# Key norms, bonus sums, merge banks and gate blocks of a hybrid decoder block put in another order on one core

## The chip, the cores and the metric

The kernel runs on one core of one Trainium2 chip. The metric is the time of one execution on the device, in microseconds (us); the median of several runs is compared. The engines of a core have a queue of instructions each and meet at semaphores: TensorE (PE, matmuls; its weight loads are PEld), VectorE (DVE), ScalarE (ACT), GpSimd (POOL), and SyncE (SP), on whose queue this kernel issues its DMAs.

## What is computed

A decoder block for 1024 tokens of width 1024. A conditioning vector gives shift, scale and gate for two sub-layers. The first sub-layer runs two token mixers on one normalised input and merges them by gates; the second is a SwiGLU feed-forward part.

```python
ada = (c @ ada_w[l] + ada_b[l])[:, None, :]
shift1, scale1, gate1, shift2, scale2, gate2 = jnp.split(ada, 6, axis=-1)
h = rms_norm(x, norm1_gain[l]) * (1 + scale1) + shift1
proj = jnp.einsum('bsd,de->bse', h, w_in[l])
rwkv_cols = proj[..., :q_lo]
rwkv_cols = rwkv_cols + (token_shift(rwkv_cols) - rwkv_cols) * tshift_mu[l]
y_a = rwkv7_time_mix(rwkv_cols, ...)
y_b = sliding_window_sink_attention(...)
gates = jax.nn.sigmoid(proj[..., g_lo:] + branch_gate_b[l])
merged = gate_a * (y_a @ w_branch_a[l]) + gate_b * (y_b @ w_branch_b[l])
x = x + gate1 * (merged @ w_out[l])
h2 = rms_norm(x, norm2_gain[l]) * (1 + scale2) + shift2
x = x + gate2 * ((jax.nn.silu(h2 @ ffn_w1[l]) * (h2 @ ffn_w3[l])) @ ffn_w2[l])
```

Inside the recurrent mixer (8 heads of 64 channels), the part that the change touches first:

```python
kk = heads(k * k_k).astype(f32)
kk = kk / jnp.maximum(jnp.sqrt(jnp.sum(kk * kk, axis=-1, keepdims=True)), 1e-12)   # key norm
k = k * (1 + (a - 1) * k_a)
y = wkv7_scan(rh, heads(decay), kh, vh, -kk, kk * ah)
bonus = jnp.sum((rh * kh * r_k).astype(f32), axis=-1, keepdims=True) * vh.astype(f32)
return (yn + bonus).reshape(B_, S_, W).astype(cols.dtype) * g
```

## The kernel before

Matrix products of float32 data are made of three matmuls on a high and a low part (`mm3`, L140 to L144). A weight block is loaded and split by `load_split`: `whi` on ACT (L133), `wlo` on VectorE (L134).

The tokens are worked on in two halves (h=0 and 1) of 512. In each half four recurrent *units* (p=0 to 3, two heads each) are formed, then an attention projection and four attention blocks, and 16 *gate blocks* (L945 to L951): a projection block of 24 matmuls, a tanh `gt` on ACT, and a store to `gates_d`, whose issue stands on SP.

A unit takes three projection blocks of 24 matmuls each, in the order k, r, v. `shifted` (L483) ends each: `tm` on ACT (L489), `rvk` on VectorE (L491). Then `rwkv_unit` (L494) is written out:

- `pz` and `paa` on PE (L499, L505), `sz` and `ath` on ACT, a scan `cum` on VectorE (L511), `wpad` and `winv` on ACT (L515, L517): the decays.
- The key norm: the square `sq` on ACT (L522), the column sum `ns` on PE (L524), `nrow` on ACT, two short DMAs by way of `n_scr`, and a reciprocal `inv2`, which the solve reads.
- `ar`, `aw`, `kp` and `kb` on VectorE (L538 to L554), with a copy of half of `kb` on ACT (L555).
- `rk`, written into the tile of `ath` (L558); the bonus sum `bs` on PE (L561) and its product with v, `bv` (L563), which only the end of the unit reads.
- The matmuls `pa` (L574), which read `kb` and `ar`; transposes `pk` and `pvt`; a triangular solve on VectorE (L605 to L625), and a loop over eight chunks (L659 to L701).

`ns`, `bs` and `pa` all write PSUM tiles of the pool `pm`, which has two buffers.

Behind each unit, `ada_rest` (L875) forms an eighth of what is left of the conditioning: eight rounds of a DMA of weights (issued on SP, L883), a product `adaw` on ACT (L884) and a sum on POOL (L885). All rounds use one buffer (`adaw2`, bufs=1), so a round's DMA is issued when POOL has done with the round before.

After the mixers, `branch` projects the two mixers' outputs and merges them with the gates, read back from `gates_d` into tiles also named `gt`. Its banks come from `pg2` (6 buffers); `psg` (L976) is a small product that spreads a gate of the conditioning, in `pn2` (2 buffers). The feed-forward part works by sums of blocks; `hidden_first` (L1272) is the first step for a pair of hidden columns: the weights are split into `wpart` (`split`, L1052), two products, and copies `u` on ACT (L1278).

A scheduler decides the order of instructions on each engine, by its own model of their times and the program's order; code under `tc.high_priority()` is put ahead of what stands before it where its data allow. The queues then run in that order.

Of the kernel before, what the change touches and what calls it, by code (L numbers as in the profile page):

```python
# [19 lines left out]
P = 128  # L20
# [7 lines left out]
NPOOL = 3  # L28
NC = HALF // 64
# [37 lines left out]
def block_kernel(ctx: ExitStack, tc: tile.TileContext, a: dict, out: bass.AP):  # L67
# [109 lines left out]
    with ExitStack() as mx:  # L177
# [316 lines left out]
        def rwkv_unit(h, p, rvk, xwa, sgx):  # L494
# [25 lines left out]

            sq = wk.tile([P, HALF], F32, tag="early", name="sq", bufs=5)
            nc.scalar.activation(out=sq, in_=k_, func=AF.Square, scale=vcol("k_k", p))  # L522
            ns = pm.tile([2, HALF], F32, tag="pm", name="ns")
            nc.tensor.matmul(ns, lhsT=blk1[:, 0:P:64], rhs=sq, start=True, stop=True)  # L524
            nrow = wk.tile([2, HALF], F32, tag="early", name="nrow", bufs=5)
            nc.scalar.copy(out=nrow, in_=ns)
            nc.sync.dma_start(out=n_scr[h, p], in_=nrow)
            inv2 = wk.tile([P, 32], F32, tag="inv2", name="inv2", bufs=2)
            nc.sync.dma_start(out=inv2, in_=n_scr[h, p].rearrange("q (c t) -> (q c) t", t=32)
                              .unsqueeze(0).broadcast_to([4, 32, 32]))  # L530
            nc.vector.tensor_scalar(out=inv2, in0=inv2, scalar1=1e-24, scalar2=None, op0=ALU.max)
            nc.vector.reciprocal(out=inv2, in_=inv2)
# [35 lines left out]
            for b in range(2):  # L568
# [325 lines left out]

        for h in range(NH):
            if h == 0:
# [20 lines left out]
            for p in range(NP):  # L917
                mixer_step(h, p, hT)
                rvk = wk.tile([P, 3, HALF], F32, tag="rvk", name="rvk", bufs=2)
                for i, j in ((2, 4 + p), (0, p), (1, 8 + p)):  # L920
                    shifted(hT, j, rvk[:, i, :])
                rwkv_unit(h, p, rvk, xwa, sgx)
# [4 lines left out]
                ada_rest(4 * h + p)  # L927

# [16 lines left out]
            for j in range(16):  # L945
                ps = proj_block(hT, 20 + j)
                gt = mw.tile([P, HALF + 1], F32, tag="tm", name="gt", bufs=3)

                nc.scalar.activation(out=gt[:, 0:HALF], in_=ps, func=AF.Tanh, scale=0.5,
                                     bias=hbg[:, j:j + 1])  # L950
                nc.sync.dma_start(out=gates_d[h, j], in_=gt[:, 0:HALF])  # L951
# [3 lines left out]
    with ExitStack() as fx:  # L955
        wp2 = fx.enter_context(tc.tile_pool(name="wp2", bufs=1))
        xp = fx.enter_context(tc.tile_pool(name="xp", bufs=1))
        wsets[:] = [wsets[0], wsets[0], (wp2, "2", 1, 1)]
        pg = fx.enter_context(tc.tile_pool(name="pg2", bufs=6, space=PSUM))
        pn = fx.enter_context(tc.tile_pool(name="pn2", bufs=2, space=PSUM))  # L960
# [252 lines left out]
        ysa[1] = load_y(ya_d, 1, lambda: st_tile("yst"))  # L1213
# [40 lines left out]
        def product(ps, w, bs, first, last):  # L1254
            hi, lo = split(w)
# [88 lines left out]
        def first(jp):  # L1344
            return hidden_first(jp, load13(jp))[0]
# [124 lines left out]
```

## Time and profile before

| what | value |
|---|---|
| timed runs | 1656.13, 1649.59, 1655.84 us, median 1655.84 |
| the profiled execution | 1638.24 us, span 1636.5 us |
| granted TensorE clock, mean | 0.989 |
| PE, PEld, DVE, ACT, POOL busy | 95%, 73%, 73%, 43%, 10% of the span |

The span is the profiled program on the core, the time has a little around it. [...] An idle time is put down to the semaphore that came last.

### The profile page before, as it was taken

How to read it: one execution, taken by the hardware profiler on the slowest of the kernel's cores; microseconds unless marked ns; L12 is line 12 of the kernel's file. 1: busy time of each engine (PE TensorE's matmuls, PEld its weight loads, DVE VectorE, ACT ScalarE, POOL GpSimd, SP SyncE). 2: the span in 40 equal slices, each digit the busy share in tenths (PEclk: the TensorE clock that was granted, in tenths of full speed). 3: DMA queues.
4: the chain of work that ended last, by engine and by line, in shares of the span. 5: the costliest groups of instructions: out<-in, count | busy, mean ns of one | idle time of the engine just before them, and what ended most of it. 6: DMA issues, size and time to landing. Idle time of an engine off the chain costs nothing.

```text
span 1636.5 us, 24815 instructions
## 1 busy us (share of the span) xinstructions
PE 1553.0 (95%) x8835; PEld 1195.9 (73%) x8835; DVE 1192.2 (73%) x2844; ACT 709.1 (43%) x1346; POOL 156.1 (10%) x220
## 2 busy tenths in 40 slices
PE   3978999999998999999999998999999999999998
PEld 2756776666665678667778886788888888888887
DVE  6689777877557868877368877976666677897465
ACT  6454343555744333446411566423333333444442
POOL 6223121212343000000000000000000000000000
PEclk9999999999999999999999999999999999999999
DMA  9345444544544323324583146253333232974441
GB/s 320 101 120 146 123 139 121 155 128 145 152 139 112 85 69 95 99 86 146 167 282 119 59 157 223 87 171 104 103 97 104 97 102 94 313 242 131 149 142 52
DMA packets 225502, 223.97 MB, mean 137 GB/s; under 512 B 38466, under 2 KB 162508, under 8 KB 225380
## 3 DMA queue, kind: packets, MB, share of 16 engines
q1 hardware_dynamic: 225380, 222.41, 44.4%
q8 instruction: 69, 1.13, 0.3%
q14 instruction: 53, 0.43, 0.1%
HBM read 171.73 MB, written 50.63 MB: 136 GB/s over the span
## 4 chain that ended last, share of the span: by engine, by line
PE 73%; DVE 11%; DMA 6%; ACT 4%; issue 2%; POOL 2%; SPq 1%; ACTq 0%; DVEq 0%; POOLq 0%
PE pgf L142 10%; PE pgf L143 10%; PE pgf L144 10%; PE pgo L144 6%; PE pgo L143 6%; PE pgo L142 6%; DMA adaw<-in_ada_w_dram 4%; PE pg L142 4%; PE pg L143 4%; PE pg L144 4%; PE pgq L142 1%; PE pgq L144 1%; PE pgq L143 1%; DVE rt L623 1%; DVE tmpi L619 1%
## 5 line engine op out<-in xcount | busy, mean ns | idle before, releaser
L142 PE MATMUL pg<-hhi,wlo 128*128 128x512 f32 x480 | 201.0, 421 | 2.0 <-DVE xwa L491 0.9
L143 PE MATMUL pg<-hlo,whi 128*128 128x512 f32 x480 | 198.8, 414 | 0.0
L144 PE MATMUL pg<-hhi,whi 128*128 128x512 f32 x480 | 198.2, 413 | 0.0
L144 PE MATMUL pgo<-wpart 128*128 128x512 f32 x420 | 163.9, 390 | 0.0
L143 PE MATMUL pgo<-wpart 128*128 128x512 f32 x420 | 163.8, 390 | 0.0
L142 PE MATMUL pgo<-wpart 128*128 128x512 f32 x420 | 163.3, 390 | 0.0
L133 ACT CAST whi<-wraw 128x1024 fp32r<-128x1024 f32 (+1 forms) x88 | 85.0, 967 | 98.2 <-PE pgf L144 45.0
L134 DVE TENSOR_TENSOR wlo<-wraw,whi 128x1024 fp32r<-128x1024 f32 (+1 forms) x88 | 100.9, 1146 | 26.0 <-ACT whi L133 18.0
L885 POOL TENSOR_TENSOR aacc<-aacc,adaw 128x512 f32<-128x512 f32 x64 | 90.6, 1416 | 257.6 <-ACT adaw L884 246.8
L142 PEld LDWEIGHTS pg<-hhi,wlo 128*128 128x128 f32 x480 | 92.5, 193 | 28.4 <-issue 6.7
L1066 DVE TENSOR_TENSOR u<-pgf,u 128x512 f32<-128x512 f32 x88 | 60.5, 689 | 68.0 <-PE pgf L144 67.1
L144 PEld LDWEIGHTS pg<-hhi,whi 128*128 128x128 f32 x480 | 92.8, 193 | 22.2 <-issue 3.3
L143 PEld LDWEIGHTS pg<-hlo,whi 128*128 128x128 f32 x480 | 92.9, 193 | 19.2 <-issue 1.3
L1061 ACT CAST wpart<-s 128x512 fp32r<-128x512 f32 x88 | 54.7, 622 | 111.0 <-PE pgf L144 99.8
L1061 ACT CAST wpart<-fo 128x512 fp32r<-128x512 f32 x77 | 48.0, 624 | 113.9 <-PE pgo L144 107.9
L1062 DVE TENSOR_TENSOR wpart<-fo,wpart 128x512 fp32r<-128x512 f32 x77 | 52.8, 687 | 52.4 <-ACT wpart L1061 52.3
L143 PEld LDWEIGHTS pgo<-wpart 128*128 128x128 f32 x420 | 78.8, 188 | 16.3 <-issue 0.2
L144 PEld LDWEIGHTS pgo<-wpart 128*128 128x128 f32 x420 | 78.9, 188 | 16.2
L142 PEld LDWEIGHTS pgo<-wpart 128*128 128x128 f32 x420 | 78.8, 188 | 16.2
L1061 ACT CAST wpart<-wraw 128x512 fp32r<-128x512 f32 x66 | 40.6, 622 | 101.3 <-PE pgf L144 98.6
L619 DVE SCALAR_TENSOR_TENSOR tmpi<-ai,inv,rt 128x60 f32<-128x60 f32 (+24 forms) x248 | 74.3, 300 | 10.6 <-DMA ai<-a_scr 6.9
L884 ACT ACTIVATE adaw<-adaw,vT 128x512 f32<-128x512 f32 x64 | 46.2, 722 | 73.2 <-DMA adaw<-in_ada_w_dram 67.7
(507 smaller groups left out, 3807.3 us busy)
## 6 DMA issues: line engine op xcount, KB each, us to landing
wraw<-in_w_in_dram SPq DMA_DIRECT2D x72, 512.0 KB
wraw<-in_ffn_w_dram SPq DMA_DIRECT2D x56, 512.0 KB
f_d<-fs SPq DMA_DIRECT2D x77, 256.0 KB
fo<-f_d SPq DMA_DIRECT2D x77, 256.0 KB
adaw<-in_ada_w_dram SPq DMA_DIRECT2D x64, 256.0 KB
w2t<-in_ffn_w_dram SPq DMA_DIRECT2D x44, 256.0 KB
adaw<-in_ada_w_dram SPq DMA_DIRECT2D x8, 1024.0 KB
gates_d<-gt SPq DMA_DIRECT2D x32, 256.0 KB
```

Source lines behind the costliest of these rows:

```text
L133: nc.scalar.copy(out=hi, in_=raw)
L134: nc.vector.tensor_tensor(out=lo, in0=raw, in1=hi.bitcast(F32), op=ALU.subtract)
L142: nc.tensor.matmul(ps, lhsT=ll, rhs=rh, start=first, stop=False, skip_group_check=more)
L143: nc.tensor.matmul(ps, lhsT=lh, rhs=rl, start=False, stop=False, skip_group_check=more)
L144: nc.tensor.matmul(ps, lhsT=lh, rhs=rh, start=False, stop=last, skip_group_check=more)
L619: nc.vector.scalar_tensor_tensor(out=tv, in0=ai[:, jj, j + 1:32].unsqueeze(1).broadcast_to([P, m, n]), scalar=inv2[:, j:j + 1], in1=rt[:, ...
L623: nc.vector.tensor_tensor(out=rt[:, 0:m, j + 1:32], in0=rt[:, 0:m, j + 1:32], in1=tv, op=ALU.add)
L884: nc.scalar.activation(out=wt, in_=wt, func=AF.Copy, scale=vcol("c", k))
L885: nc.gpsimd.tensor_tensor(out=acc, in0=acc, in1=wt, op=ALU.add)
L1061: nc.scalar.copy(out=hi, in_=src)
L1062: nc.vector.tensor_tensor(out=lo, in0=src, in1=hi.bitcast(F32), op=ALU.subtract)
L1066: nc.vector.tensor_tensor(out=out, in0=x, in1=y, op=op)
```

## The change

Five things are done, and the instructions stay the same in number and kind.

1. The square of the keys (`key_square`) is written right behind the k projection, and the rest of the key norm (`key_norm`) behind the r projection, ahead of v and of `rwkv_unit`.
2. `bs` and `bv` are written behind the loop of `pa`.
3. Three gate blocks of h=0 are written between units: one behind unit p=0, two behind p=1 (`GATES_BETWEEN`); the other 13 stay where they were.
4. The PSUM pool `pn2` is opened ahead of `pg2`, which swaps their banks.
5. In the merge, the load and split of `ysa[1]`, and in the first hidden step of the first three column pairs the splits and the `u` copies, are put under `high_priority`.

```diff
+GATES_BETWEEN = ((1, 2, 0, 0), (0, 0, 0, 0))
...
+        def key_square(p, k_):
+
+            sq = wk.tile([P, HALF], F32, tag="early", name="sq", bufs=5)
+            nc.scalar.activation(out=sq, in_=k_, func=AF.Square, scale=vcol("k_k", p))
+            return sq
+
+        def key_norm(h, p, sq):
+
+            ns = pm.tile([2, HALF], F32, tag="pm", name="ns")
+            nc.tensor.matmul(ns, lhsT=blk1[:, 0:P:64], rhs=sq, start=True, stop=True)
+            nrow = wk.tile([2, HALF], F32, tag="early", name="nrow", bufs=5)
+            nc.scalar.copy(out=nrow, in_=ns)
+            nc.sync.dma_start(out=n_scr[h, p], in_=nrow)
+            inv2 = wk.tile([P, 32], F32, tag="inv2", name="inv2", bufs=2)
...
+            nc.vector.reciprocal(out=inv2, in_=inv2)
+            return inv2
+
+        def rwkv_unit(h, p, rvk, xwa, sgx, inv2):
...
-            bs = pm.tile([P, HALF], F32, tag="pm", name="bs")
-            nc.tensor.matmul(bs, lhsT=blk1, rhs=rk, start=True, stop=True)
-            bv = wk.tile([P, HALF], F32, tag="bv", name="bv", bufs=2)
-            nc.vector.tensor_tensor(out=bv, in0=v_, in1=bs, op=ALU.mult)
...
+            bs = pm.tile([P, HALF], F32, tag="pm", name="bs")
+            nc.tensor.matmul(bs, lhsT=blk1, rhs=rk, start=True, stop=True)
+            bv = wk.tile([P, HALF], F32, tag="bv", name="bv", bufs=2)
+            nc.vector.tensor_tensor(out=bv, in0=v_, in1=bs, op=ALU.mult)
             for q in range(2):
                 for b in range(2):
                     u0 = 64 * (1 - q) + 32 * b
...
+        def gate(h, hT, j):
+            ps = proj_block(hT, 20 + j)
+            gt = mw.tile([P, HALF + 1], F32, tag="tm", name="gt", bufs=3)
+
+            nc.scalar.activation(out=gt[:, 0:HALF], in_=ps, func=AF.Tanh, scale=0.5,
+                                 bias=hbg[:, j:j + 1])
+            nc.sync.dma_start(out=gates_d[h, j], in_=gt[:, 0:HALF])
...
-                for i, j in ((2, 4 + p), (0, p), (1, 8 + p)):
-                    shifted(hT, j, rvk[:, i, :])
-                rwkv_unit(h, p, rvk, xwa, sgx)
+                shifted(hT, 4 + p, rvk[:, 2, :])
+                sq = key_square(p, rvk[:, 2, :])
+                shifted(hT, p, rvk[:, 0, :])
+                inv2 = key_norm(h, p, sq)
+                shifted(hT, 8 + p, rvk[:, 1, :])
+                rwkv_unit(h, p, rvk, xwa, sgx, inv2)
...
+                for _ in range(GATES_BETWEEN[h][p]):
+                    gate(h, hT, len(done))
+                    done.add(len(done))
...
+        pn = fx.enter_context(tc.tile_pool(name="pn2", bufs=2, space=PSUM))
         pg = fx.enter_context(tc.tile_pool(name="pg2", bufs=6, space=PSUM))
-        pn = fx.enter_context(tc.tile_pool(name="pn2", bufs=2, space=PSUM))
...
-        ysa[1] = load_y(ya_d, 1, lambda: st_tile("yst"))
+        with tc.high_priority():
+            ysa[1] = load_y(ya_d, 1, lambda: st_tile("yst"))
...
+            with tc.high_priority() if urgent else nullcontext():
+                hi, lo = split(w)
...
+                with tc.high_priority() if urgent else nullcontext():
+                    nc.scalar.copy(out=u[i], in_=ps[i])
+                product(ps[i], ws[i][2], B["21"], False, True, urgent)
...
-            return hidden_first(jp, load13(jp))[0]
+            return hidden_first(jp, load13(jp), True)[0]
```

The scheduler turns this into another order on each engine. The line numbers of the changed kernel are some 1 to 28 higher. First ACT's queue in h=0, unit p=0, from the first tanh of the unit to the copy of `kb`. Before:

```order
L501 ACTIVATE sz<-pz,hw_119 128x512
L507 ACTIVATE ath<-paa,ha_118 128x512
L210 ACTIVATE junk,nss<-xs 128x512
L884 ACTIVATE adaw_1308<-adaw_1308,vT_67 128x512
L515 ACTIVATE wpad<-cum 128x8x64
L517 ACTIVATE winv<-cum 128x512
L522 ACTIVATE sq<-rvk,vT_68 128x512
L526 COPY nrow<-ns 2x512
L489 ACTIVATE tm<-pg,vT_67 128x512
L133 CAST whi<-wraw 128x1024
L884 ACTIVATE adaw_1312<-adaw_1312,vT_67 128x512
L555 COPY kb<-kb 64x8x64
```

In the changed kernel, where `sq` stands one row ahead of this piece:

```order
L892 ACTIVATE adaw_1308<-adaw_1308,vT_67 128x512
L522 ACTIVATE sz<-pz,hw_119 128x512
L528 ACTIVATE ath<-paa,ha_118 128x512
L536 ACTIVATE wpad<-cum 128x8x64
L538 ACTIVATE winv<-cum 128x512
L134 CAST whi<-wraw 128x1024
L892 ACTIVATE adaw_1312<-adaw_1312,vT_67 128x512
L907 ACTIVATE gt<-pg,hbg 128x512
L892 ACTIVATE adaw_1316<-adaw_1316,vT_67 128x512
L490 ACTIVATE tm<-pg,vT_67 128x512
L134 CAST whi<-wraw 128x1024
L563 COPY kb<-kb 64x8x64
```

`sq` and `nrow` have left the stretch between `winv` and the copy of `kb`; a gate's `gt` and one more `adaw` have come into it.

Next the same queue one unit further on, h=0, p=1. Before:

```order
L501 ACTIVATE sz<-pz,hw_119 128x512
L507 ACTIVATE ath<-paa,ha_118 128x512
L210 ACTIVATE junk,nss<-xs 128x512 x2
L515 ACTIVATE wpad<-cum 128x8x64
L884 ACTIVATE adaw_1328<-adaw_1328,vT_67 128x512
L517 ACTIVATE winv<-cum 128x512
L522 ACTIVATE sq<-rvk,vT_68 128x512
L489 ACTIVATE tm<-pg,vT_67 128x512
L133 CAST whi<-wraw 128x1024
```

In the changed kernel:

```order
L522 ACTIVATE sz<-pz,hw_119 128x512
L528 ACTIVATE ath<-paa,ha_118 128x512
L536 ACTIVATE wpad<-cum 128x8x64
L892 ACTIVATE adaw_1336<-adaw_1336,vT_67 128x512
L538 ACTIVATE winv<-cum 128x512
L251 COPY xst<-pxt 128x512
L134 CAST whi<-wraw 128x1024
L251 COPY xst<-pxt 128x512
L907 ACTIVATE gt<-pg,hbg 128x512
L892 ACTIVATE adaw_2043<-adaw_2043,vT_67 128x512
L563 COPY kb<-kb 64x8x64
```

Here too `sq` and `nrow` are gone; an `adaw` stands between `wpad` and `winv` as before, and behind them a gate's `gt` and another `adaw` stand ahead of the copy of `kb`.

Last PE's queue in h=0, p=0, at the bonus sum and the matmuls `pa` (an xN is N of a kind; `pxt` are transposes of the input for the next half). Before:

```order
L143 MATMUL pg<-hlo,whi 128x512
L144 MATMUL pg<-hhi,whi 128x512
L561 MATMUL bs<-ath,blk_463 128x512
L574 MATMUL pa<-ar,kb 128x128 x4
L142 MATMUL pg<-hhi,wlo 128x512
L143 MATMUL pg<-hlo,whi 128x512
L144 MATMUL pg<-hhi,whi 128x512
L574 MATMUL pa<-ar,kb 128x128 x4
```

In the changed kernel:

```order
L143 MATMUL pg<-hhi,wlo 128x512
L578 MATMUL pa<-ar,kb 128x128 x4
L144 MATMUL pg<-hlo,whi 128x512
L145 MATMUL pg<-hhi,whi 128x512
L143 MATMUL pg<-hhi,wlo 128x512
L144 MATMUL pg<-hlo,whi 128x512
L145 MATMUL pg<-hhi,whi 128x512
L578 MATMUL pa<-ar,kb 128x128 x8
L143 MATMUL pg<-hhi,wlo 128x512
L578 MATMUL pa<-ar,kb 128x128 x4
L248 MATMUL pxt<-ident,xs 128x128 x4
L585 MATMUL bs<-ath,blk_463 128x512
```

`bs` has gone from ahead of the first `pa` to behind the last one, between transposes.

## Rows read from the trace of the kernel before

**Rows 1.** The page: the span, and busy time, share and instructions of each engine.
```profile
span 1636.5 us, 24815 instructions
...
PE 1553.0 (95%) x8835; PEld 1195.9 (73%) x8835; DVE 1192.2 (73%) x2844; ACT 709.1 (43%) x1346; POOL 156.1 (10%) x220
```

**Rows 2.** Busy time by stretch: us, then PE, PEld, DVE, ACT, POOL, PEclk, DMA.
```profile
75.00:270.00 195.00, 178.66 (x1366) 130.66 (x1364) 161.84 (x497) 94.44 (x172) 49.48 (x64) 0.97 0.46 127
...
450.00:655.00 205.00, 192.95 (x1445) 142.13 (x1444) 148.17 (x432) 78.74 (x143) 32.45 (x49) 0.98 0.36 100
...
975.00:1060.00 85.00, 77.83 (x345) 59.35 (x344) 69.56 (x135) 53.30 (x98) 0.00 (x0) 0.98 0.52 167
1060.00:1630.00 570.00, 570.00 (x2516) 471.98 (x2515) 404.71 (x632) 208.26 (x351) 0.00 (x0) 1.00 0.42 136
```

**Rows 3.** The list of waits of PE: us in total, times, longest.
```profile
PE ns L524 <- ACT sq L522: 16.2, 6, 6.1
...
PE bs L561 <- DVE ath L558: 6.2, 5, 3.0
...
PE sc L827 <- DVE klo L803: 4.3, 1, 4.3
PE pgf L142 <- ACT u L1278: 2.9, 2, 2.2
PE pgf L142 <- DVE wpart L1062: 2.7, 2, 1.7
...
PE psg L976 <- issue: 1.8, 1, 1.8
...
PE pgf L142 <- ACT gt L949: 1.3, 1, 1.3
```

**Rows 4.** Timeline of PE, second unit: start, us, instruction, idle before.
```profile
119.51 1.86 PE L524 MATMUL ns<-sq,blk 128*2 128x512 f32 x2 [6.13 <-ACT sq L522]
```

**Rows 5.** Timeline of ACT, second unit and first attention block.
```profile
117.61 0.72 ACT L884 ACTIVATE adaw<-adaw,vT 128x512 f32<-128x512 f32 x1 [4.17 <-DMA adaw<-in_ada_w_dram]
118.23 0.61 ACT L517 ACTIVATE winv<-cum 128x512 f32<-128x512 f32 x1
118.75 0.70 ACT L522 ACTIVATE sq<-rvk,vT 128x512 f32<-128x512 f32 x1
...
285.03 0.72 ACT L884 ACTIVATE adaw<-adaw,vT 128x512 f32<-128x512 f32 x1 [4.82 <-DMA adaw<-in_ada_w_dram]
285.65 0.51 ACT L802 CAST kdup<-pkT 64x128 fp32r<-64x128 f32 x2
```

**Rows 6.** Timelines of PE and ACT, h=1, p=2: `pz` and the last part of `kb`.
```profile
534.86 0.69 PE L499 MATMUL pz<-xwa,diu 64*128 64x512 f32 x1
...
549.02 0.62 ACT L555 COPY kb<-kb 64x512 f32<-64x512 f32 x1 [2.57 <-DVE kb L554]
```

**Rows 7.** Windows behind three waits of PE, columns as above.
```profile
118.00:124.80 6.80, 5.29 (x10) 2.90 (x11) 6.62 (x16) 4.26 (x7) 2.94 (x3) 0.50 0.15 44
162.40:165.70 3.30, 3.30 (x9) 2.32 (x8) 3.30 (x14) 0.00 (x0) 0.00 (x0) 0.50 0.18 66
507.20:513.80 6.60, 4.24 (x8) 2.05 (x9) 6.42 (x16) 3.02 (x6) 2.63 (x3) 0.50 0.39 117
```

**Rows 8.** The list of waits of ACT.
```profile
ACT adaw L884 <- DMA adaw<-in_ada_w_dram: 67.7, 36, 5.0
```

**Rows 9.** Timeline of PE, third unit, starts of matmuls of 512 columns.
```profile
163.56 0.63 PE L144 MATMUL pg<-hhi,whi 128*128 128x512 f32 x1
...
164.84 0.63 PE L144 MATMUL pg<-hhi,whi 128*128 128x512 f32 x1
...
165.97 0.39 PE L144 MATMUL pg<-hhi,whi 128*128 128x512 f32 x1
...
166.67 0.39 PE L144 MATMUL pg<-hhi,whi 128*128 128x512 f32 x1
```

More of the change, by code (lines that the diff above doesn't have):

```diff
@@ L1 @@
 import math
-from contextlib import ExitStack
+from contextlib import ExitStack, nullcontext
 from fractions import Fraction
@@ L492, in shifted @@
                                                in1=tm[:, 0:HALF], op0=ALU.mult, op1=ALU.add)
-        def rwkv_unit(h, p, rvk, xwa, sgx):
+        def key_square(p, k_):
[9 more added lines that the diff above has]
+            inv2 = wk.tile([P, 32], F32, tag="inv2", name="inv2", bufs=2)
+            nc.sync.dma_start(out=inv2, in_=n_scr[h, p].rearrange("q (c t) -> (q c) t", t=32)
+                              .unsqueeze(0).broadcast_to([4, 32, 32]))
+            nc.vector.tensor_scalar(out=inv2, in0=inv2, scalar1=1e-24, scalar2=None, op0=ALU.max)
+            nc.vector.reciprocal(out=inv2, in_=inv2)
+            return inv2
+        def rwkv_unit(h, p, rvk, xwa, sgx, inv2):
             r_, v_, k_ = (rvk[:, i, :] for i in range(3))
@@ L519, in rwkv_unit @@
             nc.gpsimd.tensor_copy(wend, wpad[:, :, 64])
[L521 to L532, printed above, removed]
             ar = wk.tile([P, NC, 2, 64], F32, tag="ar", name="ar", bufs=2)
@@ L893, in mixer_step @@
                     attention_block(4 * h + b)
+        def gate(h, hT, j):
[4 more added lines that the diff above has]
+            nc.sync.dma_start(out=gates_d[h, j], in_=gt[:, 0:HALF])
         for h in range(NH):
+            done = set()
             if h == 0:
@@ L945, in block_kernel @@
             for j in range(16):
[L946 to L951, printed above, removed]
+                if j not in done:
+                    gate(h, hT, j)
         ysb.append(load_y(yb_d, 1, stage))
@@ L1252, in load13, with product @@
             return res
-        def product(ps, w, bs, first, last):
-            hi, lo = split(w)
+        def product(ps, w, bs, first, last, urgent=False):
+            with tc.high_priority() if urgent else nullcontext():
+                hi, lo = split(w)
             for k in range(4):
@@ L1270, in f_new, with hidden_first @@
             return xp.tile([P, HALF], F32, tag="st", name="fs", bufs=7)
-        def hidden_first(jp, ws):
+        def hidden_first(jp, ws, urgent=False):
             ps, u = [bank(), bank()], []
             for i in range(2):
-                product(ps[i], ws[i][0], B["11"], True, True)
+                product(ps[i], ws[i][0], B["11"], True, True, urgent)
             for i in range(2):
                 u.append(temp("u2"))
-                nc.scalar.copy(out=u[i], in_=ps[i])
-                product(ps[i], ws[i][2], B["21"], False, True)
+                with tc.high_priority() if urgent else nullcontext():
+                    nc.scalar.copy(out=u[i], in_=ps[i])
+                product(ps[i], ws[i][2], B["21"], False, True, urgent)
             return u, gated(ps[0], ps[1], A11, jp)
```

## The prediction

> **What bounds the kernel now.** I read the page first [rows 1]. TensorE (PE) is busy 1553.0 us of a span of 1636.5; VectorE has 73%, ScalarE (ACT) 43%, GpSimd 10%. No matmul is added or taken away, so a change of order can win only from PE's 83.5 us of idle time and from stretches in which PE runs at a lower clock. The windows by stage [rows 2] say where the idle time is: the last 570 us of the feed-forward part are busy for 570.00, so nothing is to be had there. The two stretches in which mixer units are formed (75 to 270 and 450 to 655) have 195.00 - 178.66 = 16.3 and 205.00 - 192.95 = 12.1 us, the end of the merge and the first hidden blocks (975 to 1060) 85.00 - 77.83 = 7.2.
>
> The list of PE's waits [rows 3] names the owners. The key norm's matmul `ns` waits for the square `sq` on ACT six times, 16.2 us together; the bonus sum `bs` waits for the product `rk` (written into tile `ath`) five times, 6.2 us. Together that is 22.4 of the 28.4 us in those two stretches. Outside them stand one 4.3 us wait of the first attention scores, and small ones around the merge: `u` 2.9, `wpart` 2.7, `psg` 1.8, `gt` 1.3.
>
> Why `sq` is late shows in ACT's timeline [rows 5]. ACT takes its instructions in the order of its queue: `adaw` at 117.61 had stood idle for 4.17 us, until a DMA brought its weights, and `winv` and `sq`, which need nothing from that DMA, follow it at 118.23 and 118.75. PE's timeline shows the matmul `ns` right behind, after 6.13 us of idle [rows 4]. The conditioning stream has one buffer (`adaw2`, bufs=1), so ACT waits for it 36 times, 67.7 us in all, at most 5.0 us [rows 8]. It is therefore not the arithmetic of the norm that costs, but whatever PE needs from ACT behind an `adaw`.
>
> A stall has a second price. [...] Three matmuls of 512 columns after each other take 164.84 - 163.56 = 1.28 us there and 166.67 - 165.97 = 0.70 us when it is over [rows 9], 0.427 and 0.233 us each, so each microsecond of PE work in such a window would have taken 0.55: the loss is 0.45 of the busy time, 5.29 x 0.45 = 2.4, 3.30 x 0.45 = 1.5 and 4.24 x 0.45 = 1.9 us, together 5.8.
>
> **The change part by part.** *Key norm early.* `sq` needs only the k projection, and in the new order it stands behind that block's `tm` on ACT; `ns` stands on PE behind the r projection of 24 matmuls, at least 24 x 0.233 = 5.6 us after the end of the k block, in most units over 10 us. At most one `adaw` stands between. A wait of the longest kind (5.0) is thus just covered, so I set the six waits to nothing: **-16.2**; the bound on the other side is one wait left over, +5. The two short DMAs of the norm (n_scr, inv2) go out earlier by the same amount, and only the solve needs their result, far behind: nothing.
>
> *Bonus sum late.* `bs` waited because it ends a chain: `pz`, `sz`, the scan, `winv`, `aw`, `kp`, `kb`, `rk`. Now it stands behind the `pa` matmuls and reads long finished data: **-6.2**. But `pa` needs `kb`, whose last part, the copy on ACT, is the end of nearly the same chain. Before, `pa` was free because `bs` had waited for it. So the wait moves to `pa`, and its size is what PE has to do between `pz` and `pa` against the length of the chain. I counted the new order, at 0.233 us for 512 columns and some 1.1 for `pz` and its sister `paa`: in h=0 unit 0, 36 matmuls (9.6 us); unit 1, 45 and eight transposes (13.3); h=1 unit 0, 35 and part of an attention block (12.7); h=1 unit 1, 45 (11.6); in the four others 19.7 us or more (long stretches of attention work stand between). The chain was shortest in h=1 unit 2: from `pz` at 534.86 to the copy's end at 549.02 + 0.62 = 549.64, 14.8 us [rows 6]. Against 14.8 the four units lack 5.2 + 1.5 + 2.1 + 3.2 = **+12.0**. The bounds: nothing, if VectorE, now without the norm between, runs the chain in under 10 us; and +24 if one `adaw` wait of 3 us (between none and 5.0) comes on top in each of the four. The order gives reason for the latter: in unit 0 two `adaw` now stand ahead of the copy. I stay at the middle value, and add **+4** of half clock for these waits, two of which are as long as the one that cost 1.5 [rows 7]. The half clock behind the old waits goes: **-5.8**.
>
> *Three gate blocks between units.* A gate block is 24 matmuls (5.6 us), a tanh on ACT and a DMA issue on SP, which waits there for the tanh. As cover for unit 0's and unit 1's chains the blocks are already in the counts above. Where they came from, the attention blocks of h=0, 13 are left of 16 to fill gaps. On ACT no `adaw` stands directly ahead of `kdup` in the first attention block any more; before, one held it for 4.82 us [rows 5], and the scores waited 4.3 plus about 1.5 of half clock. Of these 5.8 I take **-4**, since `klo` on VectorE is also in that chain; bounds 0 and -5.8. For cover that is now missing elsewhere, and for new places of `adaw` in other units, I put **+5**, an estimate of one `adaw` wait; bounds 0 and 15 (three of them).
>
> *Merge.* The banks laid anew let `psg`, which waited 1.8, stand six blocks into the stage and free the first banks sooner than the gate `gt` that held them for 1.3; the splits and copies of the first hidden blocks come earlier in the queues of ACT and VectorE (`wpart` 2.7, `u` 2.9). These four waits are 8.7 in all [rows 3]. Eight hidden-state activations still stand ahead of `u` on ACT, so part of that stays: I take **-6**, bounds 0 and -10 with the clock.
>
> [...] The 6.1 us that `ns` cost in unit 1 came from strict order on ACT [rows 5], and the new order has more `adaw` ahead of `kb` than before. [...]
>
> **Sum.** -16.2 - 6.2 - 5.8 + 12.0 + 4 - 4 + 5 - 6 = -17.2 us. The profiled execution took 1638.24 us (span 1636.5 and 1.7 around it), so it would take 1621.0, a ratio of 0.9895. The median of the three timed runs is 1655.84, 1.1% above the profiled one; I carry the ratio over: 1655.84 x 0.9895 = **1638 us**.
>
> **The rivals.** *Mixed, as summed* (1638; with its widest term, the wait of `pa` and its clock, at its bounds of 16 less and 12 more, 1622 to 1650): chance 0.56.
>
> *One for one:* `pa` takes over what `ns` and `bs` left, since all three hang on the same ACT queue; only the merge part, 6 us, remains: about 1650. For it speaks that PE did less work between `pz` and `pa` in the new order in four units than the chain needs; against it, that the four other units are covered. Chance 0.19.
>
> *Slower:* the copy of `kb` waits for a full `adaw` round in every unit, beyond what the work covers. Place: ACT, rows between `winv` and the copy. Price: 5.0 plus about 2 of half clock in eight units is 56 us, beside the 16.2 + 6.2 + 5.8 + 10 = 38 saved: +18, about 1674. It decides from 38/8 = 4.8 us per unit on. Against it speaks that the one copy shown waited for VectorE and not for an `adaw`, 2.57 us [rows 6], and that in four units the cover is about 20 us or more. Chance 0.10.
>
> *All goes and nothing takes its place:* the chain without `sq`, `nrow` and `ns` gets under 10 us. Then -16.2 - 6.2 - 5.8 - 5.8 - 9 = -43, about 1612. Chance 0.15. For it speaks that two instructions of ACT and a matmul leave the stretch between `winv` and `aw`; against it, VectorE's 73% and the solve of the unit before in the same queue.
>
> **From cases to numbers.** A measurement of this kernel can tell about 0.5%, 8.3 us, from no change. Faster than 1647.6: nearly all of the mixed case (0.53), all of the last (0.15) and a little of the one for one case (0.04): 0.72. Within 0.5% is the rest of these, 0.03 and 0.15: 0.18. Slower by more: 0.10. The range runs from 1612, where all waits are gone, to 1654, beyond the one for one case; the slower case and a little on the lower side are left out, 0.15 together. The likeliest case alone has 1622 to 1650.
>
> **What would show it.** In the changed kernel's list of PE waits `ns` <- `sq` should be gone or under 2 us, `bs` too, and a new line `pa` <- ACT `kb` should stand with 8 to 20 us, in units 0 and 1 of each half (p=0 and 1). If `kb` copies start right behind an `adaw` with a DMA wait in ACT's timeline, the one for one or slower case is on. The windows at 0.50 behind `ns` and `bs` [rows 7] should be gone, and one or two new ones stand behind `pa`. `psg`, `wpart`, `u` should fall from 8.7 to about 3 with `gt`. I would be wrong if PE's idle time outside the units grew (attention of h=0, with three gate blocks fewer), or if a wait showed on PE that has no line now, such as one for the weights' DMA behind a gate's store on SP.

## The result: 0.6% slower, and the profile after

The changed kernel takes 1660.03 us in the median of 10 runs, the kernel before 1649.74 in 10 beside it; the ratio is 1.0061, with an interval of 1.0032 to 1.009. Forecast was 1638, a ratio of 0.9895. The profiled execution of the changed kernel has a span of 1661.5 us and a mean granted clock of 0.971, where that of before had 0.989. Its page, the rows that answer to [rows 1]:

```profile
span 1661.5 us, 24797 instructions
...
PE 1569.8 (94%) x8835; PEld 1204.7 (73%) x8835; DVE 1195.3 (72%) x2844; ACT 708.8 (43%) x1346; POOL 157.0 (9%) x220
```

PE's idle time is 1661.5 - 1569.8 = 91.7 us, 8.2 more than before, and PE's busy time has grown by 16.8 us, although not one matmul was added. The second number is the larger: the same matmuls took longer, and the windows below show PE at half clock for longer. The list of PE's waits, which answers to [rows 3]:

```profile
PE pv L652 <- DVE tn L646: 9.5, 3, 4.9
PE pxt L248 <- DVE xs L218: 7.9, 1, 7.9
PE pa L578 <- DVE rt L631: 6.6, 1, 6.6
...
PE pgf L144 <- DVE y_0l L165: 4.0, 1, 4.0
...
PE pgf L143 <- ACT u L1301: 2.0, 2, 1.3
PE pgf L143 <- DVE mg L1042: 2.0, 1, 2.0
...
PE pgf L143 <- DVE wpart L1082: 1.0, 1, 1.0
PE psg L996 <- DMA yst<-ya_d: 1.0, 1, 1.0
...
PE pa L578 <- DVE kb L562: 0.8, 2, 0.4
```

The lines `ns` <- `sq` and `bs` <- `ath` are gone, as forecast, 22.4 us less. `pa` <- `kb`, which I had expected with 8 to 20 us, has 0.8. But five waits stand there that the kernel before did not have at this size: `pv`, a matmul behind the solve, for `tn` 9.5; `pxt`, transposes of the input, for `xs` 7.9; `pa` for the solve's `rt` 6.6; and in the merge `y_0l` 4.0 and `mg` 2.0. Together they are 30.0 us. In the merge `psg`, `wpart`, `u` and `gt` went from 8.7 to 4.0, so the edits there did what they say and were paid for right beside.

One of these waits, followed through the four engines (timelines of SP's queue, ACT, VectorE and PE in the second unit):

```profile
106.19 0.47 SPq L242 DMA_DIRECT2D xs<-in_x_dram  x1
...
116.84 0.63 ACT L211 ACTIVATE junk<-xs 128x512 f32<-128x512 f32 x1 [6.54 <-DMA xs<-in_x_dram]
...
126.59 0.75 DVE L218 TENSOR_SCALAR xs<-xs,nxn 128x1024 f32<-128x1024 f32 x1
...
127.39 0.47 PE L248 MATMUL pxt<-ident,xs 128*128 128x128 f32 x1 [7.87 <-DVE xs L218]
```

SP issues the load of `xs` at 106.19. ACT's next instruction in its queue, the sum of squares `junk`, waits 6.54 us for it; behind it stand `tm`, `whi` and `sz` of the unit. VectorE gets to the norm of `xs` only at 126.59, between steps of the solve, and PE, which has run through a gate block and the projections almost without a stop, stands before the transposes `pxt` for 7.87 us. The new order brought PE to this place earlier than VectorE could. Without the gate blocks (e1 below) SP issues the same load at 103.06, and `pxt` has no wait there.

The windows at half clock, readings of 0.50 to 0.52 where 1.00 is full speed (columns as in [rows 2]):

```profile
122.50:132.50 10.00, 5.11 (x14) 4.10 (x15) 9.76 (x25) 3.71 (x6) 3.60 (x6) 0.50 0.45 131
166.50:183.50 17.00, 16.66 (x118) 9.64 (x118) 10.64 (x30) 7.38 (x14) 4.73 (x6) 0.50 0.30 89
...
334.50:344.50 10.00, 10.00 (x90) 7.02 (x86) 4.95 (x16) 5.30 (x12) 1.79 (x2) 0.52 0.34 107
...
559.80:569.80 10.00, 10.00 (x90) 7.11 (x90) 6.34 (x17) 4.42 (x8) 2.85 (x3) 0.52 0.46 145
```

In the whole execution the mean clock of 0.971 is a share of 2 x 0.029 of the span at half clock, 96 us; in that of before it was 2 x 0.011, 36 us. This takes the clock to stand at 1.00 or 0.50 and nowhere else: of 1386 windows of 0.5 us in the first 700 us, 1374 read one of the two before and 1372 after. Two of the windows, 334 and 560, have PE busy for the full 10.00 us: no wait is seen within them.

**A way to part the two.** Time lost to the clock can be read from any run, since each has its mean granted clock c: a share 2 x (1 - c) of it ran at half clock, and by the rate of the prediction (0.45 of the busy time [rows 7, 9]) that cost 0.9 x (1 - c) of the time. What is left I call the time at full clock. That it is a fair estimate shows in 106 runs of the kernel before, with 106 different times, taken beside the experiments on five chips: they spread from 1634.83 (c = 0.989) to 1659.32 us (c = 0.973), and at full clock these two are 1618.6 and 1619.0; all 106 are 1620.4 with a standard deviation of 2.1, against 5.7 of the times themselves. So nearly all of the spread of one and the same program goes with its clock. For the change this says: time at full clock 1620.4 before and 1619.0 after (-1.4); lost to the clock 26.1 before and 40.8 after (+14.7). Slow runs are left out throughout, of the kernel before five of 1659.47 to 1662.86 us.

The split is no better than some 5 us where the clock is low. It charges the clock also for half-clock time in which PE stands still (in the first window above PE is busy for 5.11 of 10.00 us), and a line through the 106 runs has 0.79 in the place of 0.9. With 0.8 the change is at +0.3 and +13.0, and e5 below at +5.9 and +39.7 instead of +0.9 and +44.7. In the two profiled executions PE's idle time has grown by 8.2 us, which the estimate doesn't show.

### The profile page after: what moved, and what is told of

Same layout as the page of the kernel before. It is cut to its first block, busy times and chain, and to the rows that moved or that the text cites. A ratio compares the mean times of both kernels' runs of the same rounds, so it can differ in the third digit from the quotient of the medians.

```text
span 1661.5 us, 24797 instructions
## 1 busy us (share of the span) xinstructions
PE 1569.8 (94%) x8835; PEld 1204.7 (73%) x8835; DVE 1195.3 (72%) x2844; ACT 708.8 (43%) x1346; POOL 157.0 (9%) x220
## 4 chain that ended last, share of the span: by engine, by line
PE 72%; DVE 13%; DMA 7%; ACT 3%; issue 2%; SPq 1%; POOL 1%; ACTq 0%; DVEq 0%; POOLq 0%
PE pgf L145 9%; PE pgf L144 9%; PE pgf L143 9%; PE pgo L144 6%; PE pgo L143 6%; PE pgo L145 6%; PE pg L145 5%; PE pg L143 4%; PE pg L144 4%; DMA adaw<-in_ada_w_dram 2%; DMA ai<-a_scr 2%; DVE tmpi L627 1%; DVE wlo L135 1%; PE yps L708 1%; PE pgq L144 1%
## 5 line engine op out<-in xcount | busy, mean ns | idle before, releaser
L145 PE MATMUL pg<-hhi,whi 128*128 128x512 f32 x480 | 203.1, 423 | 0.0
L144 PE MATMUL pg<-hlo,whi 128*128 128x512 f32 x480 | 202.2, 421 | 0.0
L893 POOL TENSOR_TENSOR aacc<-aacc,adaw 128x512 f32<-128x512 f32 x64 | 86.9, 1358 | 248.5 <-ACT adaw L892 235.3
L627 DVE SCALAR_TENSOR_TENSOR tmpi<-ai,inv,rt 128x60 f32<-128x60 f32 (+24 forms) x248 | 78.3, 316 | 27.0 <-DMA ai<-a_scr 22.8
```

Of the source, the lines that this page charges most:

```text
L144: nc.tensor.matmul(ps, lhsT=lh, rhs=rl, start=False, stop=False, skip_group_check=more)
L145: nc.tensor.matmul(ps, lhsT=lh, rhs=rh, start=False, stop=last, skip_group_check=more)
L627: nc.vector.scalar_tensor_tensor(out=tv, in0=ai[:, jj, j + 1:32].unsqueeze(1).broadcast_to([P, m, n]), scalar=inv2[:, j:j + 1], in1=rt[:, ...
L893: nc.gpsimd.tensor_tensor(out=acc, in0=acc, in1=wt, op=ALU.add)
```

## The experiments

Where an experiment's text names the time at full clock, it is this estimate. All results in one table; the ratio is that of the times, with its interval, against runs of the kernel before on the same chip. The last two columns are means over the runs.

| kernel | median us | ratio | at full clock | lost to clock |
|---|---|---|---|---|
| before | 1646.6 (106 runs) | 1 | 1620.4 | 26.1 |
| the change | 1660.0 | 1.0061 (1.0032 to 1.009) | 1619.0 | 40.8 |
| e1 no gates | 1654.7 | 1.0038 (1.0006 to 1.0069) | 1612.9 | 42.5 |
| e2 merge alone | 1653.9 | 1.0021 (0.999 to 1.0052) | 1622.6 | 29.6 |
| e3 norm and bonus | 1648.4 | 1.0002 (0.9969 to 1.0035) | 1611.1 | 36.5 |
| e4 gates alone | 1660.8 | 1.0082 (1.0051 to 1.0112) | 1623.2 | 37.4 |
| e5 norm alone | 1691.4 | 1.0276 (1.0237 to 1.0314) | 1621.3 | 70.8 |
| e6 bonus alone | 1630.0 | 0.9903 (0.9872 to 0.9933) | 1609.4 | 21.3 |
| e7 e1 without the priority of ysa[1] | 1651.9 | 1.0032 (1.0002 to 1.0062) | 1614.6 | 38.6 |
| e8 e3 with more matmuls | 1683.9 | 1.0201 (1.0152 to 1.025) | 1637.7 | 42.0 |
| e9 e3, reciprocal late | 1656.0 | 1.0047 (1.002 to 1.0073) | 1613.5 | 41.6 |
| e10 bonus and banks | 1632.1 | 0.9913 (0.9879 to 0.9947) | 1610.0 | 21.5 |
| e11 bonus and priorities | 1632.8 | 0.9916 (0.9887 to 0.9946) | 1612.6 | 20.9 |
| e12 bonus and gates | 1647.1 | 1.0001 (0.9974 to 1.0029) | 1617.8 | 29.0 |
| e13 before, adaw on POOL | 1690.3 | 1.0284 (1.0258 to 1.0309) | 1639.4 | 53.6 |
| e14 bonus, adaw on POOL | 1676.2 | 1.019 (1.0158 to 1.0222) | 1630.6 | 47.1 |
| e15 norm and bonus, adaw on POOL | 1694.6 | 1.0291 (1.0265 to 1.0316) | 1629.8 | 65.3 |
| e16 the change, adaw on POOL | 1703.1 | 1.034 (1.0317 to 1.0363) | 1641.1 | 61.3 |
| e17 bonus, product left out | 1641.6 | 0.9955 (0.9923 to 0.9986) | 1610.8 | 31.8 |
| e18 norm and bonus, product left out | 1651.7 | 1.0033 (1.0002 to 1.0064) | 1611.3 | 41.7 |

**The parts, first cut.** My theory was that the gate blocks cost (G); the rivals were the norm and the bonus themselves (N) and the merge (M).

```diff
 # e1: the change, but
-GATES_BETWEEN = ((1, 2, 0, 0), (0, 0, 0, 0))
+GATES_BETWEEN = ((0, 0, 0, 0), (0, 0, 0, 0))
 # e2: before, with the banks, the priority of ysa[1] and the urgent splits alone
 # e3: before, with key_square and key_norm early and bs behind pa alone
 # e4: before, with GATES_BETWEEN = ((1, 2, 0, 0), (0, 0, 0, 0)) alone
```

e1. 

> The whole change without the three gate blocks between units. Theory G (the gate blocks are what costs: with them, TensorE reaches transposes of the input and the solve's matmuls before VectorE has their data, 7.9 + 6.6 + 9.5 us of waits and the half clock behind them): these waits shrink to under 8 us in all and the time is 1.0% under before, about 1633 us. Theory N (forming the norm early and the bonus late is itself what lets TensorE run into the solve): the waits stay, and the time is as of the changed kernel, 0.6% over before. Theory M (the merge part costs: y_0l 4.0, mg 2.0 and half clock behind): merge is slow as in the changed kernel, some 8 us longer than before, the rest is won, so about 0.3% under before.

e2. 

> The kernel before with the merge part alone (banks, priority for the load of ysa[1], priority for the first splits). The order up to the merge is that of before. Theory M: the stage from the first merge matmul to the first of the output projection is 104 instead of 96 us, and the time 0.5% over before. Theories G and N: the merge's loss in the changed kernel came from what ran late into it, so here the time is the same or up to 0.4% less.

e3. 

> The kernel before with the key norm early and the bonus sum late alone. Theory G: ns and bs waits are gone (22 us and 6 of half clock), nothing of size in their place: 1.0% under before. Theory N: new waits pv <- tn, pxt <- xs or pa <- rt of 15 us and more and longer half clock in their place: 0 to 1% over before.

e4. 

> The kernel before with the three gate blocks between units alone. Theory G: 0.5 to 1.5% over before, with pxt <- xs among the waits. Theory N: the same as before within 0.4%, since the gate blocks only fill.

Measured: e4 alone is 0.8% slower, as G said. But e3 is no faster than before (1.0002), which G had put at 1.0% under, and taking the gates out of the change (e1) leaves it 0.4% over. So G is only a part. e3's waits on PE:

```profile
PE pa L578 <- DVE kb L562: 6.1, 2, 4.1
PE pv L652 <- DVE tn L646: 6.1, 3, 3.0
...
PE pg L143 <- DVE wlo L135: 4.8, 3, 3.2
...
PE yps L704 <- DVE ar L548: 2.9, 1, 2.9
```

These four are 19.9 us, in the place of 22.4 that left: the time at full clock is 9.3 us under before by the estimate, and the clock takes it back with 10.4. How a weight comes late there, in the second unit (timelines of ACT, VectorE and PE):

```profile
116.09 0.73 ACT L892 ACTIVATE adaw<-adaw,vT 128x512 f32<-128x512 f32 x1 [3.10 <-DMA adaw<-in_ada_w_dram]
...
118.33 1.03 ACT L134 CAST whi<-wraw 128x1024 fp32r<-128x1024 f32 x1
...
119.76 0.17 DVE L511 TENSOR_SCALAR inv<-inv 128x32 f32<-128x32 f32 x1
...
121.70 1.16 DVE L135 TENSOR_TENSOR wlo<-wraw,whi 128x1024 fp32r<-128x1024 f32 x1
...
122.92 0.50 PE L143 MATMUL pg<-hhi,wlo 128*128 128x512 f32 x1 [3.16 <-DVE wlo L135]
```

ACT waits 3.10 us in `adaw` and casts `whi` only at 118.33; VectorE takes `inv` of the early norm, and besides it `ar`, `rvk` and steps of the solve, before it comes to `wlo` at 121.70; PE has stood for 3.16 us when it goes on at 122.92. In the kernel before PE had stood for 6.13 us until 119.51, for `sq`, behind the same `adaw` [rows 4, 5].

e2 shows the merge's new wait without anything else changed, since its order is that of before up to the merge. PE's waits, then VectorE's and PE's timelines:

```profile
PE pgf L144 <- DVE y_0l L165: 5.1, 1, 5.1
```

```profile
877.10 0.69 DVE L1086 TENSOR_TENSOR t4o<-wo,t2o 128x512 f32<-128x512 f32 x1
877.71 0.68 DVE L165 TENSOR_TENSOR y_0l<-yst,y_0h 128x512 fp32r<-128x512 f32 x1
...
878.45 0.79 PE L144 MATMUL pgf<-y_0l,whi 128*128 128x512 f32 x1 [5.05 <-DVE y_0l L165]
```

`y_0l`, the low half of the other branch's input, stands on VectorE behind a run of block sums (`t4o`), and PE waits 5.05 us. The stage from the first merge matmul to the first of the output projection is 917.98 - 815.56 = 102 us against 904.75 - 808.59 = 96. In time it is not clear of nothing (0.999 to 1.0052). Theory M is right on the wait, and its loss of 0.5% lies within the interval, as no loss at all does.

**Norm and bonus apart.**

```diff
 # e5: before, with key_square and key_norm early alone
 # e6: before, with bs and bv behind the loop of pa alone
 # e7: e1, but
-        with tc.high_priority():
-            ysa[1] = load_y(ya_d, 1, lambda: st_tile("yst"))
+        ysa[1] = load_y(ya_d, 1, lambda: st_tile("yst"))
```

e5. 

> The kernel before with the key norm early alone. To part waits from clock, each run's time is taken times 1 - 0.9 x (1 - its mean granted clock), the time at full clock: 1620.6 for the kernel before, 1611.1 with norm and bonus together. Theory N1 (the norm carries the gain, the bonus has nothing to add, since kb ends the same chain): 1609 to 1613 at full clock, with bs <- ath of 6 to 12 us among the waits. Theory N2 (the waits of ns only pass to bs, as long as bs stands ahead of pa): 1617 to 1621, and bs <- ath of 15 us or more.

e6. 

> The kernel before with the bonus sum late alone. Theory N1: ns keeps its 16 us, bs loses 6 and pa gets them: at full clock 1617 to 1622, within 0.3% of before in time. Theory N2: bs late is what frees PE: 1611 to 1615 at full clock.

e7. 

> Norm, bonus, banks and the priority of the first splits, but not the priority of the load of ysa[1] (and no gate blocks between). Theory Y (the priority of that load makes the wait y_0l of 5.7 us and the half clock behind it): the wait is gone, at full clock 1605 to 1609 instead of 1612.9, and the half clock in the merge under 4 us; the time is 0.3 to 0.6% under that of the version with it. Theory B (the banks are what brings it): the wait stays, time and clock as with it.

This was the decisive cut, and both theories missed it. The bonus alone is 1.0% faster: 11.0 us at full clock and 4.8 of clock. The norm alone is 2.8% slower, by the estimate with 0.9 us more at full clock and 44.7 us more lost to the clock. The profiled execution of e5 (span 1689.5 us) bears out that the clock has most of it: its PE row, and a window with columns as in [rows 2]:

```profile
PE 1596.7 (95%) x8835; PEld 1223.3 (72%) x8835; DVE 1200.5 (71%) x2844; ACT 709.3 (42%) x1346; POOL 151.2 (9%) x220
...
208.20:249.10 40.90, 39.77 (x273) 27.22 (x273) 22.76 (x69) 15.62 (x32) 7.90 (x8) 0.50 0.19 56
```

The same 8835 matmuls take 43.7 us more than in [rows 1]. PE's idle time is 1689.5 - 1596.7 = 92.8 us, 9.3 more than before, so a part of the loss is waits after all. The longest stretch at half clock lasts 41 us with PE busy for 39.77 of 40.90.

At full clock N2 is the nearer one on both kernels (1617 to 1621 for e5, 1611 to 1615 for e6). But `bs` in e5 waits 3.0 us and not 15 or more: other waits stand in the place of those of `ns` (`pv` <- `tn` 12.3, `pg` <- `wlo` 7.3, `y_0l` 5.5), which neither had named. PE's waits in e6:

```profile
PE ns L504 <- ACT sq L498: 9.3, 6, 3.9
...
PE pa L579 <- DVE kb L563: 4.4, 3, 2.6
```

`ns` itself is smaller here than in [rows 3] (9.3 against 16.2), and `pa` waits 4.4 us: less than the 12.0 of my sum. e7 did not bear out theory Y: without the priority `y_0l` still waits 2.8 us, and the time is not clear of e1's.

**Banks and priorities on top of the bonus, and the gates.**

```diff
 # e10: e6, and pn2 opened ahead of pg2
 # e11: e6, and high priority for ysa[1] and for the splits and copies of first()
 # e12: e6, and
+GATES_BETWEEN = ((1, 2, 0, 0), (0, 0, 0, 0))
```

e10. 

> The bonus sum late and the banks of the merge, no more. The order up to the merge is that of the bonus alone (1609.4 at full clock, median 1630 us). Theory B (the banks bring the wait y_0l): y_0l of 3 to 6 us, the merge's first stage about 8 us longer, 1611 to 1614 at full clock. Theory P (the priorities bring it): no y_0l, 1607 to 1610.

e11. 

> The bonus sum late and the merge's priorities (load of ysa[1], first splits and copies), no more. Theory B: no y_0l, and u and wpart shrink from 5.6 to under 4, so 1606 to 1609 at full clock and a time at or just under that of the bonus alone. Theory P: y_0l of 3 to 6 us and 1611 to 1614.

e12. 

> The bonus sum late and the three gate blocks between units, no more. Theory G (gate blocks between units cost whatever is around them): 5 us or more over the bonus alone at full clock, 1614 to 1618, with pxt <- xs or pv <- tn of 5 us among the waits. Theory N (they cost only with the norm early, whose wait for a DMA on VectorE the added work does not cover): 1606 to 1610, and a time within 0.3% of the bonus alone.

Banks and priorities, each by itself, leave the time of the bonus alone within the measurement (0.9913 and 0.9916 against 0.9903); at full clock the banks give 0.6 and the priorities 3.2 more, the latter with a `y_0l` of 2.4 us (theory P, at a small size). The priorities are not its only cause: e5 has neither banks nor priorities, and a `y_0l` of 5.5. The gates cost 1.0% on top of the bonus, 8.4 us at full clock and 7.7 of clock, so G holds where the norm is not early too. PE's waits in e12:

```profile
PE ns L504 <- ACT sq L498: 8.3, 3, 5.7
...
PE pv L653 <- DVE tn L647: 6.1, 1, 6.1
...
PE pxt L248 <- DVE xs L218: 5.6, 2, 4.6
...
PE pgq L144 <- DVE wlo L135: 5.0, 3, 3.7
```

`tn`, `xs` and `wlo` are on VectorE, and `ns` is still there: the gate blocks gave PE work, but these waits stand beside it.

**Is it the reciprocal, or small matmuls that stand together?**

```diff
 # e8: e3, and ahead of the transposes into pk, pvt and pyt
+            for _ in range(2):
+                nc.tensor.matmul(ps.rearrange("p c v -> p (c v)"), lhsT=hT[0][0][:, 0:P], rhs=hT[0][0],
+                                 start=True, stop=True)
 # e9: e3, and the maximum and reciprocal of inv2 moved from key_norm to just ahead of the tile rt
```

e8. 

> Norm and bonus alone, and two matmuls of 128x512 more into each of the banks pk, pvt and pyt ahead of their transposes, which overwrite them: 96 matmuls of work that is thrown away, 22 us at full clock. Theory D (the clock falls where small matmuls of 64 columns stand together without large ones, wait or no wait): the half clock shrinks from 81 us to under 50, and the time rises by 5 to 15 us instead of 22. Theory W (the clock falls only behind waits): the half clock stays at 75 to 90 us, and the time rises by 20 us or more, less what the waits give.

e9. 

> Norm and bonus as in the change, but the maximum and the reciprocal of the norm, VectorE's two instructions that wait for the short DMA, are written behind the transposes, right ahead of the solve that reads them; no gate blocks, merge as before. Theory V (the early norm puts a wait for a DMA into VectorE's queue, inv 5.0 us, and so makes kb, wlo and tn late): inv disappears from VectorE's waits, pa <- kb, pg <- wlo and pv <- tn shrink from 17 us to under 9, at full clock 1605 to 1608 instead of 1611.1, and the time 0.5 to 1% under before. Theory R (the early norm costs by the early matmul ns and the moved k, r, v blocks, whatever VectorE does): the waits stay, 1610 to 1613 at full clock, same time as before.

e8: the 96 matmuls cost 26.6 us at full clock, and the clock's loss did not shrink (42.0 against 36.5); that is 93 us at half clock, more than either theory had. Theory D, that small matmuls alone bring the clock down, is not borne out; but the scheduler also laid the rest anew around them, so W is not shown either. e9: theory V falls. `inv` still waits 2.9 us on VectorE, `tn` 8.1 and `ar` 5.5 on PE, and the kernel is 0.5% slower than before, where V had it faster.

**Is it `adaw` in ACT's queue?** This is the cause that my prediction had named for `ns`.

```diff
 # e13 to e16: before, e6, e3 and the change, with
-                nc.scalar.activation(out=wt, in_=wt, func=AF.Copy, scale=vcol("c", k))
+                nc.gpsimd.tensor_scalar(out=wt, in0=wt, scalar1=vcol("c", k), scalar2=None,
+                                        op0=ALU.mult)
 # e17, e18: e6 and e3, with
-                nc.scalar.activation(out=wt, in_=wt, func=AF.Copy, scale=vcol("c", k))
```

e13. 

> The kernel before, with the product adaw on GpSimd instead of ScalarE (same result). Theory A (the waits of ns, and those that replace them, hang on adaw in ScalarE's queue): ns <- sq falls from 16 to under 5 us, at full clock 1605 to 1612 instead of 1620.3, and the time 0.5 to 1% under before. Theory O (the order of the matmuls against a chain on VectorE is what counts): ns keeps 10 us or more, 1617 to 1622, time within 0.4%.

e14. 

> The bonus sum late, adaw on GpSimd. Theory A: 1600 to 1606 at full clock instead of 1609.4, ns under 4 us, and the fastest or second fastest of all. Theory O: 1608 to 1611.

e15. 

> Norm early and bonus late, adaw on GpSimd. Theory A: pg <- wlo, pa <- kb and pv <- tn fall from 17 us to under 8, 1600 to 1606 at full clock, no slower than the bonus alone on GpSimd by over 0.2%; the early norm then costs nothing. Theory O: it stays 0.7% or more slower than the bonus alone.

e16. 

> The whole change, adaw on GpSimd. Theory A: 1.0% or more faster than the change with adaw on ScalarE (1660 us), so 1643 or less. Theory O: within 0.5% of it.

e17. 

> The bonus sum late; the multiplication of the conditioning weights by c on ScalarE is left out (64 instructions of 0.72 us), so the later parts of the conditioning are not those of the reference. Theory A (the waits hang on that product's wait in ScalarE's queue): ns falls from 9.3 to under 4 us, at full clock 1602 to 1607 instead of 1609.4. Theory O (the order of matmuls against VectorE's chain): ns stays at 7 us or more, 1608 to 1612.

e18. 

> Norm early and bonus late, the same multiplication left out. Theory A: pg <- wlo, pa <- kb and pv <- tn together under 8 us instead of 17, at full clock 1602 to 1607, and the cost of the early norm (1.0% in time against the bonus alone) falls to 0.3% or less against its sister. Theory O: these waits stay over 12 us, and the early norm still costs 0.7% or more.

On GpSimd everything is 1.9 to 3.4% over before, outside of both theories. The groups of POOL's instructions in e14 (busy, mean ns | idle before), and a row of VectorE's timeline:

```profile
L893 POOL TENSOR_SCALAR adaw<-adaw,vT 128x512 f32<-128x512 f32 x64 | 107.7, 1683 | 166.4 <-DMA adaw<-in_ada_w_dram 166.0 <-POOL carry L491 0.2
```

```profile
509.86 1.23 DVE L532 TENSOR_TENSOR_SCAN cum<-cmask,sz 128x512 f32<-128x512 f32 x1 [13.28 <-POOL sz L523]
```

The product takes 1.68 us there instead of 0.72, and waits 166 us for its DMAs in a queue that also holds `sz`; the scan `cum` then stands 13.28 us for `sz`. The wait had only been carried to another queue, so these four don't tell the theories apart. e17 does. Without the product ACT never waits for these weights, and the waits of PE are:

```profile
PE ns L504 <- ACT sq L498: 11.7, 6, 3.6
...
PE pa L579 <- DVE kb L563: 4.4, 2, 2.4
```

`ns` has 11.7 us, where theory A had under 4 and e6 had 9.3, and the time at full clock is 1610.8 against 1609.4, as theory O had both. In time e17 is 0.5% under before, and not 1.0% as e6, since it loses 10.5 us more to the clock. One of the six waits of `ns` (timelines of ACT and PE, h=1, second unit):

```profile
522.35 0.63 ACT L536 ACTIVATE wpad<-cum 128x512 f32<-128x512 f32 x1 [2.76 <-DVE cum L532]
...
523.40 0.71 ACT L498 ACTIVATE sq<-rvk,vT 128x512 f32<-128x512 f32 x1
...
524.16 1.21 PE L504 MATMUL ns<-sq,blk 128*2 128x512 f32 x2 [1.96 <-ACT sq L498]
```

`wpad` stands ahead of `sq` in ACT's queue and waits 2.76 us for VectorE's scan `cum`; it does so ahead of all six, for 0.81 to 2.76 us, and ahead of the longest ACT waits 2.90 us for a load of `xs` besides. So the `adaw` that stands ahead of `sq` in [rows 5] is the last to end in that place, but not what decides: without it the scan of the same unit ends last. In e18 PE's waits are:

```profile
PE yps L704 <- DVE ar L548: 5.8, 2, 3.5
...
PE pg L143 <- DVE wlo L135: 3.8, 2, 3.2
...
PE pa L578 <- DVE kb L562: 1.9, 1, 1.9
PE pv L652 <- DVE tn L646: 1.7, 3, 1.3
```

The three waits that theory A named are down to 7.4 us as it said, where O had over 12; but `yps` <- `ar` has 5.8, and the time at full clock is 1611.3, not under 1607. e18 against e17, on the same chip, is the cost of the early norm once more: 1651.7 against 1641.6 us, 0.6% (0.8% by the two ratios), some 0.5 us at full clock and 9.9 of clock. A had 0.3% or less, O 0.7% or more. So theory A falls as the cause of `ns` and of the early norm's cost, and is right on where `wlo`, `kb` and `tn` came from. That the order of PE against the chains on VectorE and ACT decides, as O has it, fits e17; as the account of the whole it is argued and not shown.

**What the clock did with one order.** e2 has the order of before up to the merge, so the two executions can be compared there. Windows around 220 us: before, then e2 (PE busy, PEclk, DMA):

```profile
206.20:209.60 3.40, 3.40 (x53) 1.00 0.78 245
216.40:219.80 3.40, 3.40 (x38) 1.00 0.17 60
226.60:230.00 3.40, 3.19 (x31) 1.00 0.42 128
236.80:240.20 3.40, 3.40 (x37) 1.00 0.00 0
```

```profile
206.20:209.60 3.40, 3.40 (x58) 1.00 0.35 116
216.40:219.80 3.40, 3.40 (x28) 0.50 0.42 110
226.60:230.00 3.40, 3.40 (x17) 0.50 0.83 305
236.80:240.20 3.40, 3.40 (x13) 0.52 0.00 1
```

In e2 the clock falls at about 216 us and stays at 0.50 for 24 us; in the 10 us ahead of that PE ran matmuls of 32 to 256 columns and transposes, and its timeline shows no idle time of over 0.2 us; in the other execution the clock does not fall. The order of the matmuls is the same in both up to there, and so are the data; the chip may not be. Busy here is modelled, so short pauses between the small matmuls of the recurrence can hide in it.

## Why the prediction was wrong

- *The key norm: "I set the six waits to nothing: -16.2".* This is the step that failed. The six waits did go, but PE's time did not fall with them: alone the early norm gives nothing at full clock (+0.9), on top of the bonus it costs 1.7, and in the profiled execution of e5 PE's idle time is 9.3 us over before. PE waits for `wlo`, `tn`, `ar` and `kb` instead (e3, e5). I had written this down as a rival, one for one, but with `pa` as the only place where the wait could go; it went to the solve and to the weights. The sign of error that I had named, a wait on PE that had no line before, is there: `pxt` for `xs`, `pa` for `rt`.
- *The half clock: "-5.8" and "+4".* This term failed with it, and most of the time went here: +14.7 us instead of -3.3 with the 1.5 of the scores' wait, some 18 of the 27 us between the forecast and the result. I had tied the half clock to the waits in one execution [rows 7] and let it go with them. The norm alone lost some 40 to 45 us more to the clock, in part in a stretch of 41 us with hardly a wait. And the execution that I read, at 0.989, had lost 16 us by the estimate, of which I had priced 5.8; the mean of 106 runs is 26.1.
- *The bonus: "-6.2" and "+12.0" of `pa`.* The place was right and the size wrong: `pa` waits 4.4 us in e6, and `ns` shrank too. Worked as a sum, norm and bonus were set at -10.4 without the clock and measured -9.3 (e3). That this comes close is luck, for the shares are wrong: the bonus brings it all.
- *The gates: "-4" and "+5".* Measured +6.1 at full clock in the change (e1 against it) and +8.4 on top of the bonus. The scores' wait went from 4.3 to 0.9, as said; the waits that came with the gates are those of the transposes `pxt` (7.9) and of the solve's `rt` (6.6), which e1 does not have, not missing cover in the attention.
- *The merge: "-6".* The named waits fell from 8.7 to 4.0, but `y_0l` and `mg` came with 6.0. At full clock the merge part costs 1.8 to 2.2 us.
- *The strict order on ACT* [rows 5], to which I put down the 6.1 us of `ns`, and the rival one for one: the traces bear out that the wait moved (in e3 19.9 us in the place of 22.4). That `ns` waits because of `adaw` is what e17 contradicts: without it `ns` waits 11.7 us.
- The slower rival came true in sign, not in mechanism: the copy of `kb` behind `adaw` cost PE 0.5 us.

Not settled: why the early norm's order keeps the clock low for so long. That most of the loss is the clock's is shown by PE's busy time in e5, and by the estimate in e3 against e6 and in e18 against e17; what in the order brings the clock down is not shown. The change without the early norm, and a clock held high by other means, were not tried.

The versions that beat both kernels are the bonus alone, e6 (1630.0 us, 0.9903 of before, six runs), and the same with the banks or the priorities (e10 and e11, 0.9913 and 0.9916).

## What to carry to other kernels

Taking away the wait that a list names need not pay: PE can stand a little further on for the same chain, as it did here. Ask where the engine will stand next, and what it finds there. Cut a change of several parts into its parts before judging it: here one part gave 1.0%, and each of two others took it back. Where the clock moves, read each run's clock beside its time, and set a sum against many runs, not against the one that was profiled.

## What the hardware showed

- One program, 106 runs: 1634.83 to 1659.32 us, and nearly all of that spread goes with the granted clock (0.989 to 0.973); at full clock, by the estimate, their standard deviation is 2.1 us.
- The half clock lasted long in places, with PE shown as busy: 41 us in e5 (PE busy 39.77 of 40.90), 24 us in e2, 17 us in the changed kernel (166.5 to 183.5 above, PE busy 16.66 of 17.00). At 122.5 to 132.5 us of the changed kernel it began within a wait: PE stood for 7.87 us until 127.39, and the reading went from 1.00 at 120 to 122 us to 0.50 from 122.5 us on. At 216 us in e2 no such wait is shown.
- A product of 128x512 with a scalar per partition took 1.68 us on GpSimd (e14, 64 of them) and 0.72 us on ACT (before, 64 of them).
